# A two-layer hybrid network, second feed-forward: float32 of the norm kept, operands prepared in steps, phases overlapped

## The chip, the cores and the metric

The kernel runs on one core of one Trainium2 chip. The metric is device time in microseconds (us), lower is better. TensorE (PE; PEld are its weight loads), VectorE (DVE), ScalarE (ACT), GpSimd (POOL) and SyncE (SP, which issues the DMAs) run side by side, each with an in-order queue.

## What is computed

The reference is a network of two layers on 1024 latent tokens (and 256 context tokens in the first layer), width 1024. Each layer has a mixer (attention and a recurrence) and a feed-forward part. The change lies in the second layer's feed-forward part and in the norm ahead of it, both on latent tokens only:

```python
def squared_relu_mlp(u, w1, w2):
    return jnp.square(jax.nn.relu(u @ w1)) @ w2

h_l = h_l + mod_l[5] * squared_relu_mlp(
    modulate(rms_norm(h_l, norm2_w[i]), mod_l[3], mod_l[4]), w_ff1[i], w_ff2[i])
return rms_norm(h_l, final_norm_w)
```

`w_ff1` is 1024 x 4096, `w_ff2` 4096 x 1024, all float32.

## The kernel before

Activations stand with features on the 128 partitions and tokens in the free dimension. A float32 number is kept as two rounded float32 parts (hi and lo, type fp32r), and one product of 128 x 128 weights with 512 tokens is three matmuls (`mm3`, lines 132 to 134): hi by hi, hi by lo, lo by hi. Splitting takes a cast on ScalarE and a subtraction on VectorE or POOL (`split`, lines 139 and 140).

`norm_mod` (line 1222) makes the normed input of one half of the tokens (c = 0 or 1, 512 tokens): squares and their sums over eight feature tiles, a matmul with ones (line 1240) and a power on POOL (1243), transposes that spread the result over the partitions (1248), and then `mod_part` for each feature tile k: VectorE's scaling (355), ScalarE's shift that gives hi (356), and lo on VectorE (364), or, for k = 1, 3, 5, 7 of the second half, by a float32 copy (358) and POOL (362). It is a generator; other code advances it step by step, and each step appends to the engines' queues. `out_proj` advances it for the first half, and its last eight steps of squares for the second.

`ff_halves` (line 2441) then does the feed-forward part in three pieces.

- `ff` on four units (1,0,0), (1,1,0), (1,0,1), (1,1,1): an ordinary first product for 512 hidden features, each unit 48 matmuls, result squared and spilled to memory. The first unit goes through k outermost. After each half unit it advances `fills` by `rate` = 7 steps: the rest of the norm, the spilling of the residual (8 steps), and `ff_combine` (line 1460).
- `ff_first` (1504), the seven-product phase for the other hidden features (Winograd's form of Strassen's scheme): features and tokens are halved, and of four blocks of u (B11, B21, B12, B22) and four combinations (T1 to T4) seven are multiplied with seven combinations of four weight blocks. `ff_combine` makes T1 to T4: it adds hi and lo of u together on POOL (1471), forms sums on VectorE and splits them. There are 14 pairs of hidden blocks with 7 products each; a product is 12 matmuls into one PSUM bank. `weights` prepares the weight blocks, FFA = 5 ahead; `post` takes the results from PSUM in steps, makes the seven combinations of the squared hidden values and writes them to memory (`hs_d`).
- `ff_second` (1623), the seven-product phase of the second product: 7 groups of 7 products; a product is four chains of 6 matmuls, each into a bank of its own (8 banks in all). `operands` loads weights (1637) and hidden values (1645), forms the four weight sums (1662 to 1665) when a group's first operand is due, and splits both operands (`pair`). The main loop keeps FFB = 3 operands ahead. After each chain the result of the chain before it is added to U (1709) or to the residual (1716), from a list `posts`.

The last hidden features follow as ordinary products, with the final norm. The order of the work is that of emission (`manual_schedule`): what stands earlier in a queue holds up what stands behind it. Tiles come from pools: slots `S` (45 of 4 KB per partition), temporaries `T` (6), PSUM banks `P` (8).

Of the kernel before, what the change touches and what calls it, by code (L numbers as in the profile page):

```python
# [21 lines left out]
KT = 8  # L22
# [325 lines left out]

def mod_part(E, src, r, u, k, c, gain, shift, pool=False):

    nc = E.nc
    v = 0 if c < 2 else 1
    f = E.T([128, CH[c][1]])
    hi, lo = u.part(k, c, 0), u.part(k, c, 1)
    nc.vector.scalar_tensor_tensor(f, src, gain[:, k, v:v + 1], r, op0=OP.mult, op1=OP.mult)
    nc.scalar.activation(hi, f, AF.Identity, bias=shift[:, k, v:v + 1])  # L356
    if pool:
        nc.scalar.activation(f, f, AF.Identity, bias=shift[:, k, v:v + 1])
    yield
    yield  # L360
    if pool:
        nc.gpsimd.tensor_tensor(lo, f, hi.bitcast(F32), op=OP.subtract)
    else:
        nc.vector.scalar_tensor_tensor(lo, f, shift[:, k, v:v + 1], hi.bitcast(F32), op0=OP.add, op1=OP.subtract)  # L364
    yield
# [128 lines left out]
def drain(g):  # L494
    for _ in g:
        pass
# [724 lines left out]

def norm_mod(E, h, u, c, gain, shift, pool=False, lag=2, which=0):

# [26 lines left out]
    yield from pipe([mod_part(E, h.part(k, c), r[:, :n], u, k, c, gain, shift, k in MPOOL[which][c])  # L1250
                     for k in range(KT)], 1)

# [201 lines left out]
FFA = 5  # L1454
FFB = 3
B11, B21, B22, B12, T1, T2, T3, T4 = range(8)
MOVING = {1: B11, 2: B21, 3: B22, 4: T4, 5: T1, 6: T2, 7: T3}


def ff_combine(E, u, B):  # L1460

    nc = E.nc
    for b, k, c in ((B11, 0, 0), (B21, 4, 0), (B12, 0, 1), (B22, 4, 1)):
        B[b] = [u.tile(k + i, c) for i in range(4)]
    for b in (T1, T2, T3, T4):
        B[b] = []
    f32 = lambda t, i: t[:, i].bitcast(F32)

    def whole(t):
        f = E.T([128, 512], name="uf")  # L1470
        nc.gpsimd.tensor_tensor(f, f32(t, 0), f32(t, 1), op=OP.add)
        return f

    def put(b, f, pool):
        t = E.S([128, 2, 512], F32R, name="ut")
        E.split(t[:, 0], t[:, 1], f, pool=pool)
        B[b].append(t)

    for a, b in ((T1, T2), (T3, T4)):
        for k in range(4):  # L1480
            f12, f22 = whole(B[B12][k]), whole(B[B22][k])
            yield
            d = E.T([128, 512], name="ud")
            if a == T1:
                f11 = whole(B[B11][k])
                nc.vector.tensor_tensor(d, f12, f11, op=OP.subtract)
                nc.vector.tensor_tensor(f22, f22, d, op=OP.subtract)
                yield
                put(T1, d, False)
                yield  # L1490
                put(T2, f22, False)
            else:
                f21 = whole(B[B21][k])
                nc.vector.tensor_tensor(d, f22, f12, op=OP.subtract)
                yield
                put(T3, d, False)
                nc.vector.tensor_tensor(f22, f32(B[T2][k], 0), f32(B[T2][k], 1), op=OP.add)
                nc.vector.tensor_tensor(f21, f21, f22, op=OP.subtract)
                yield
                put(T4, f21, False)  # L1500
            yield


def ff_first(E, l, B, pairs, dst, fills):
# [87 lines left out]
    order = ((1, "x"), (6, "y"), (5, "z"), (7, "y"), (2, "x"), (4, "y"), (3, "z"))  # L1592
    yield
    for i, p in enumerate(pairs):
        bank = {}
# [27 lines left out]
def ff_second(E, l, groups, src, h, fills):  # L1623
# [22 lines left out]

    def pair(raw, pool):
        hi, lo = (E.S([128, 2, 512], F32R, name="sp") for _ in range(2))
        E.split(hi, lo, raw, pool=pool)
        return hi, lo  # L1650

    def operands():
        v = nc.vector
        load(0)
        for j in range(2):
            fetch(j)
        yield
        for j, (i, n) in enumerate(todo):
            if n == 1:
                a11, a21, a22, a12 = (raws.pop((i, m, z)) for m, z in ((0, 0), (0, 1), (1, 1), (1, 0)))  # L1660
                s1, s2, s4 = (E.S([128, 2, 512], name="ws") for _ in range(3))
                v.tensor_tensor(s1, a21, a22, op=OP.add)  # L1662
                v.tensor_tensor(s2, s1, a11, op=OP.subtract)  # L1663
                v.tensor_tensor(a21, a11, a21, op=OP.subtract)  # L1664
                v.tensor_tensor(s4, a12, s2, op=OP.subtract)  # L1665
                A = {1: a11, 2: a12, 3: s4, 4: a22, 5: s1, 6: s2, 7: a21}
                del a11, a12, a21, a22, s1, s2, s4
# [5 lines left out]
            o = [(w, t)]  # L1673
            del w, t
            yield o.pop()

    ops, ready, posts = operands(), [], []
    next(ops)
    yield
    U, banks, hr = {}, {}, None  # L1680
    for i, g in enumerate(groups):
        for n in order:
            while len(ready) < (1 if i == 0 and n == 1 else 2 if i == 0 and n == 2 else FFB):
                x = next(ops, None)
                if x is None:
                    break
                ready.append(x)
                x = None
            w, t = ready.pop(0)
            if n == 1 and i == 0:  # L1690
                hr = h()
            for o in range(4):
# [659 lines left out]
LAG1 = 6  # L2352
# [5 lines left out]
def kernel(ctx: ExitStack, tc: tile.TileContext, A, out, dbg=None, upto=99):  # L2358
# [57 lines left out]
    E.mark('mixer1')  # L2416
    u, W, norm = Act(E, 8), {}, []

    def tail(O, h):
        norm.extend(norm_mod(E, h, u, c, E.gain[1, 1], E.mod[1][:, 3], c == 1, (2, LAG1)[c], 2) for c in range(2))  # L2420
        return out_proj(E, 1, O, h, 0, W, None, norm[0])
# [15 lines left out]
    E.mark('ff1')  # L2437
    ff_halves(E, 1, u, h, norm[1])


def ff_halves(E, l, u, h, fill):
    nc = E.nc
# [19 lines left out]
    drain(fills[0])  # L2462
    del B[B12]
    u.t.clear()
    left = 7 * len(pairs)
    back = Back(E)

    def residual():
        for _ in range(8):
# [74 lines left out]
```

## Time and profile before

| | us |
|---|---|
| median of 3 runs | 3035.26 (3035.12 to 3037.11) |
| the profiled execution, its own time | 3036.59 |
| its span from first to last instruction | 3034.8 |
| busy: PE, DVE, ACT, POOL | 2848.8, 1837.2, 1314.1, 1250.3 |

The span is the time from the first instruction to the last in the profiled execution; times in rows count from its start. Busy time is the union of an engine's instructions. Matmuls overlap in the records (each lasts 0.39 us and the next starts 0.23 us later), so pace is read from starts and counts. "Idle before" is the time for which an engine stood still ahead of an instruction, and behind the arrow stands whose end released it. PEclk is the granted clock of TensorE as a share of 2.4 GHz.

### The profile page before, as it was taken

What the parts mean: (1) busy time and instruction counts of PE and PEld (TensorE: products, weight loads), DVE (VectorE), ACT (ScalarE), POOL (GpSimd) and SP (SyncE); (2) the same over time, 40 slices, a digit from 0 to 9 for tenths busy, and PEclk for the clock granted to TensorE, in tenths of its full rate; (3) what the DMA queues carried; (4) which work ended last, traced back from release to release, by engine and by line L of the source; (5) the groups of instructions that cost most, each with busy time, mean ns of one, the idle gap of its engine ahead of it and who ended that gap; (6) DMA issues with size and microseconds to landing.
All of it is one profiled execution on the core that took longest, in us unless ns stands there. A gap on an engine that the chain in (4) does not pass through costs nothing. (4 is left out here: it accounts for less than half of the span.)

```text
span 3034.8 us, 43217 instructions
## 1 busy us (share of the span) xinstructions
PE 2848.8 (94%) x16181; PEld 2453.1 (81%) x16181; DVE 1837.2 (61%) x3507; ACT 1314.1 (43%) x2475; POOL 1250.3 (41%) x946
## 2 busy tenths in 40 slices
PE   7999999989999999999999989899996699889998
PEld 5797789878888888888888788789885588767777
DVE  5453468876435444444445865898976655567767
ACT  5554468764112121111134444488863344433331
POOL 1443347634223223222233343335446655465560
PEclk9999999999999999999999999999998899989999
DMA  7236689821212122222214212235312344464441
GB/s 254 80 119 202 225 229 233 223 84 61 71 44 70 63 70 74 80 77 70 84 29 142 74 56 87 81 109 159 117 36 111 118 153 153 149 219 139 137 148 56
DMA packets 255801, 355.16 MB, mean 117 GB/s; under 512 B 34848, under 2 KB 160616, under 8 KB 255592
## 3 DMA queue, kind: packets, MB, share of 16 engines
q1 hardware_dynamic: 255592, 352.41, 36.5%
q8 instruction: 127, 2.08, 0.3%
q14 instruction: 82, 0.67, 0.1%
HBM read 261.05 MB, written 91.31 MB: 116 GB/s over the span
## 5 line engine op out<-in xcount | busy, mean ns | idle before, releaser
L132 PE MATMUL ps<-act,whi 128*128 128x512 f32 (+1 forms) x1728 | 630.9, 365 | 6.3 <-ACT act L356 5.2
L133 PE MATMUL ps<-act,whi 128*128 128x512 f32 (+1 forms) x1728 | 627.4, 363 | 6.2 <-DVE act L364 4.4
L134 PE MATMUL ps<-act,wlo 128*128 128x512 f32 (+1 forms) x1728 | 625.1, 362 | 2.1 <-POOL wlo L92 1.1
L92 POOL TENSOR_TENSOR wlo<-wst,whi 128x1024 fp32r<-128x1024 f32 x134 | 333.3, 2496 | 365.4 <-ACT whi L90 242.6
L132 PEld LDWEIGHTS ps<-act,whi 128*128 128x128 f32 x1728 | 329.2, 190 | 60.7 <-issue 7.6
L133 PEld LDWEIGHTS ps<-act,whi 128*128 128x128 f32 x1728 | 329.1, 190 | 55.3 <-DVE act L364 5.8
L134 PEld LDWEIGHTS ps<-act,wlo 128*128 128x128 f32 x1728 | 328.6, 190 | 53.0 <-POOL wlo L92 1.6
L140 DVE TENSOR_TENSOR hid<-t,hid 128x512 fp32r<-128x512 f32 (+1 forms) x104 | 65.5, 630 | 451.8 <-ACT hid L139 451.8
L132 PE MATMUL ps<-hid,whi 128*128 128x512 f32 (+1 forms) x848 | 301.2, 355 | 0.0
L133 PE MATMUL ps<-hid,whi 128*128 128x512 f32 (+1 forms) x848 | 299.6, 353 | 0.0
L134 PE MATMUL ps<-hid,wlo 128*128 128x512 f32 (+1 forms) x848 | 299.4, 353 | 0.0
L1348 POOL TENSOR_TENSOR t<-t 128x512 f32<-128x512 f32 (+1 forms) x104 | 95.7, 920 | 483.5 <-ACT t L1347 475.4
L1347 ACT ACTIVATE t<-ps 128x512 f32<-128x512 f32 (+1 forms) x104 | 55.3, 532 | 491.6 <-PE ps L134 491.6
L1372 DVE SCALAR_TENSOR_TENSOR hl<-ps,mod,hl 128x512 f32<-128x512 f32 (+1 forms) x296 | 208.7, 731 | 63.2 <-PE ps L134 60.1
L724 ACT ACTIVATE sc<-sc,st 128x1024 f32<-128x1024 f32 (+3 forms) x208 | 178.1, 859 | 32.1 <-DVE st L1826 23.1
L132 PE MATMUL ps<-sp,sp 128*128 128x512 f32 x392 | 161.5, 412 | 28.3 <-DVE hl L1716 23.1
L90 ACT CAST whi<-wst 128x1024 fp32r<-128x1024 f32 x138 | 142.1, 1048 | 90.4 <-PE ps L133 41.8
L753 DVE TENSOR_TENSOR pt<-ps,pt 128x512 fp32r<-128x512 f32 (+2 forms) x304 | 169.2, 598 | 17.7 <-ACT pt L752 15.2
L132 PEld LDWEIGHTS ps<-hid,whi 128*128 128x128 f32 x848 | 160.4, 189 | 24.0 <-issue 1.6
L134 PEld LDWEIGHTS ps<-hid,wlo 128*128 128x128 f32 x848 | 160.3, 189 | 22.1
L133 PEld LDWEIGHTS ps<-hid,whi 128*128 128x128 f32 x848 | 160.4, 189 | 21.5
L133 PE MATMUL ps<-sp,sp 128*128 128x512 f32 x392 | 160.1, 408 | 11.3 <-DVE sp L140 7.9
(393 smaller groups left out, 6541.4 us busy)
## 6 DMA issues: line engine op xcount, KB each, us to landing
wm<-in_w_mod SPq DMA_DIRECT2D x96, 512.0 KB
wst<-in_w_ff SPq DMA_DIRECT2D x86, 512.0 KB
hs<-hs_d SPq DMA_DIRECT2D x49, 512.0 KB
wr<-in_w_ff SPq DMA_DIRECT2D x42, 512.0 KB
hs_d<-g SPq DMA_DIRECT2D x42, 512.0 KB
hl<-h_d SPq DMA_DIRECT2D x24, 512.0 KB
wst<-in_w_in_even SPq DMA_DIRECT2D x20, 512.0 KB
wst<-in_w_in_odd SPq DMA_DIRECT2D x18, 512.0 KB
```

Of the source, the lines that this page charges most:

```text
L90: self.nc.scalar.copy(hi, st)
L92: engine.tensor_tensor(lo, st, hi.bitcast(F32), op=OP.subtract)
L132: t.matmul(ps, w[0], u[0], start=start, stop=False, **kw)
L133: t.matmul(ps, w[0], u[1], start=False, stop=False, **kw)
L134: t.matmul(ps, w[1], u[0], start=False, stop=stop, **kw)
L140: (self.nc.gpsimd if pool else self.nc.vector).tensor_tensor(lo, src, hi.bitcast(F32), op=OP.subtract)
L724: self.E.nc.scalar.activation(s, s, AF.Exp, bias=self.nm, accum_out=self.st[:, 5 + i:6 + i])
L753: nc.vector.tensor_tensor(pt[:, :, 1], src, pt.bitcast(F32)[:, :, 0], op=OP.subtract)
L1347: nc.scalar.activation(r, ps[:, :n], AF.Relu)
L1348: nc.gpsimd.tensor_tensor(r, r, r, op=OP.mult)
L1372: nc.vector.scalar_tensor_tensor(dst, ps[:, :n], gate[:, o, v:v + 1], dst, op0=OP.mult, op1=OP.add)
```

## The change

- `mod_part` and `norm_mod` take a dictionary `keep`: for the second layer the float32 value is written to a kept tile (eight slots: k and k + 4 of a half share one), the float32 shift is done for every k, and lo is the difference of the two (VectorE, or POOL as before). The order of k becomes 0, 4, 1, 5, 2, 6, 3, 7.
- `ff_combine` takes these tiles: four sums in a row on VectorE per k, then four splits, lo of T2 and T4 on VectorE, of T1 and T3 on POOL. Three steps per k.
- `fills` now also holds the first six steps of `ff_first` (loads and five weight blocks), and is advanced by FFR = 10 steps instead of 7.
- `operands` of the second phase goes in four steps per operand: cast of the weights, cast of the hidden values, lo of the weights on POOL, lo of the hidden values on POOL (first three operands of a group) or VectorE (the other four; before, POOL had the second, fourth and sixth). The four weight sums of the next group go with the second step of the group's last four operands. The main loop advances it by one step per chain, or two when fewer than FFB = 2 operands are ready.
- The first FFS = 16 steps of the second phase are issued between the last products of the first one, from the 93rd on, and the residual is loaded two tiles per chain of the first product.

```diff
-def mod_part(E, src, r, u, k, c, gain, shift, pool=False):
+def mod_part(E, src, r, u, k, c, gain, shift, pool=False, keep=None):
...
-    f = E.T([128, CH[c][1]])
+    if keep is None:
+        f = E.T([128, CH[c][1]])
+    else:
+        if k % 4 not in keep:
+            keep[k % 4] = E.S([128, 2, 512], name="uf")
+        f = keep[k % 4][:, k // 4]
...
-    if pool:
+    if pool or keep is not None:
         nc.scalar.activation(f, f, AF.Identity, bias=shift[:, k, v:v + 1])
     yield
     yield
-    if pool:
-        nc.gpsimd.tensor_tensor(lo, f, hi.bitcast(F32), op=OP.subtract)
+    if pool or keep is not None:
+        (nc.gpsimd if pool else nc.vector).tensor_tensor(lo, f, hi.bitcast(F32), op=OP.subtract)
...
     yield from pipe([mod_part(E, h.part(k, c), r[:, :n], u, k, c, gain, shift, k in MPOOL[which][c], keep)
-                     for k in range(KT)], 1)
+                     for k in (range(KT) if keep is None else (0, 4, 1, 5, 2, 6, 3, 7))], 1)
...
 FFA = 5
-FFB = 3
+FFR = 10
+FFB = 2
+FFS = 16
...
-def ff_combine(E, u, B):
+def ff_combine(E, u, F, B):
...
+    for k in range(4):
+        a, b = F[0].pop(k), F[1].pop(k)
+        f11, f21, f12, f22 = a[:, 0], a[:, 1], b[:, 0], b[:, 1]
+        d = E.T([128, 512], name="ud")
+        for o, x, y in ((f11, f12, f11), (d, f22, f11), (f12, f22, f12), (f21, f21, d)):
+            nc.vector.tensor_tensor(o, x, y, op=OP.subtract)
+        yield
+        for n, f in ((T2, d), (T1, f11), (T3, f12), (T4, f21)):
+            t = E.S([128, 2, 512], F32R, name="ut")
+            E.split(t[:, 0], t[:, 1], f, pool=n in (T1, T3))
+            B[n].append(t)
+            if n in (T1, T4):
                 yield
...
     yield
+    while len(ready) < FFA:
+        ready.append(next(ws))
+        yield
     for i, p in enumerate(pairs):
...
+        for n in range(4):
+            sums(0, n)
+            yield
         for j, (i, n) in enumerate(todo):
-            if n == 1:
...
-            if n == 5:
+            at = j % 7
+            if at == 0:
                 load(i + 1)
             fetch(j + 2)
-            w = pair(A.pop(n), True)
-            t = pair(moving.pop(j), j % 7 in (1, 3, 5))
...
+            x, y = A[i].pop(n), moving.pop(j)
+            w, t = ([E.S([128, 2, 512], F32R, name="sp") for _ in range(2)] for _ in range(2))
+            nc.scalar.copy(w[0], x)
+            yield
+            nc.scalar.copy(t[0], y)
+            if at > 2 and i + 1 < len(groups):
+                sums(i + 1, at - 3)
+            yield
+            nc.gpsimd.tensor_tensor(w[1], x, w[0].bitcast(F32), op=OP.subtract)
+            del x
+            yield
+            (nc.gpsimd if at in (0, 1, 2) else nc.vector).tensor_tensor(t[1], y, t[0].bitcast(F32), op=OP.subtract)
+            del y
+            ready.append((w, t))
...
+                if n == 1 and i == 0:
+                    hr = h()
+                if n == 1 and i == 0 or len(ready) < FFB:
+                    next(ops, None)
+                next(ops, None)
...
-    fills = [chain(fill, spill(), ff_combine(E, u, B))]
-    del h
-    first = ff_first(E, l, B, pairs, {p: hs[p // 2][:, p % 2] for p in pairs}, fills)
+    first = ff_first(E, l, B, pairs, {p: hs[p // 2][:, p % 2] for p in pairs}, [])
+    fills = chain(fill, spill(), ff_combine(E, u, F, B), islice(first, 1 + FFA))
...
-    ff(E, l, u, None, ops, fill=fills[0], spill=hd, rate=7)
+    ff(E, l, u, None, ops, fill=fills, spill=hd, rate=FFR)
...
-    next(first)
+    left, steps = 7 * len(pairs), 0
     for _ in first:
         left -= 1
-        if left == 4:
-            next(second)
+        if left < 6 and steps < FFS:
+            step(second, 3 if left < 3 else 2)
+            steps += 3 if left < 3 else 2
+    step(second, FFS - steps)
```

## Rows read from the trace of the kernel before

**Rows 1.** The page, part 1: busy time, share, instructions of each engine.

```profile
PE 2848.8 (94%) x16181; PEld 2453.1 (81%) x16181; DVE 1837.2 (61%) x3507; ACT 1314.1 (43%) x2475; POOL 1250.3 (41%) x946
```

**Rows 2.** Stretches: PE, PEld, DVE, ACT, POOL busy (instructions), PEclk, DMA share, GB/s.

```profile
2290.20:2332.90 42.70, 37.28 (x157) 29.05 (x156) 21.27 (x26) 17.12 (x28) 21.61 (x17) 0.92 0.43 172
2332.90:2376.90 44.00, 0.00 (x0) 0.00 (x0) 32.48 (x32) 10.38 (x18) 29.51 (x20) 0.54 0.22 72
2376.90:2646.40 269.50, 269.10 (x1176) 221.57 (x1176) 150.42 (x178) 128.60 (x221) 144.06 (x98) 0.99 0.44 148
2646.40:2659.10 12.70, 0.79 (x2) 0.28 (x1) 11.21 (x10) 3.14 (x4) 2.53 (x1) 0.66 0.61 215
2659.10:2707.90 48.80, 38.27 (x144) 30.38 (x144) 29.60 (x26) 22.54 (x25) 37.01 (x14) 0.85 0.76 282
2883.80:2928.20 44.40, 40.96 (x168) 33.35 (x169) 31.88 (x37) 15.21 (x16) 26.14 (x11) 0.92 0.30 99
...
2974.40:3034.80 60.40, 52.37 (x305) 45.39 (x303) 41.15 (x79) 13.34 (x41) 0.00 (x0) 0.95 0.18 70
...
2382.00:2642.00 260.00, 259.74 (x1146) 214.72 (x1146) 146.58 (x173) 124.59 (x215) 140.99 (x96) 1.00 0.45 153
```

**Rows 3.** Waits from 2290 to 2382: in total, times, longest.

```profile
PE ps L132 <- ACT sw L139: 44.0, 1, 44.0
...
PE ps L133 <- DVE act L364: 4.3, 1, 4.3
```

**Rows 4.** Timeline of PE, DVE, ACT, POOL around the first units: start, length, instruction.

```profile
2290.13 0.95 PE L1240 MATMUL ps<-one,t 128*128 128x1 f32 x8
...
2284.90 3.91 DVE L364 SCALAR_TENSOR_TENSOR act<-t,mod,act 128x512 fp32r<-128x512 f32 x2
...
2299.73 1.40 DVE L355 SCALAR_TENSOR_TENSOR t<-hl,gain,ps 128x512 f32<-128x512 f32 x2
...
2300.50 1.38 ACT L356 ACTIVATE act<-t,mod 128x512 fp32r<-128x512 f32 x2 [1.42 <-DVE t L355]
...
2292.88 1.02 POOL L1243 TENSOR_TENSOR nst<-nst,mhalf 128x4 f32<-128x4 f32 x1 [1.53 <-DVE nst L1242]
2293.87 1.04 POOL L1348 TENSOR_TENSOR t<-t 128x512 f32<-128x512 f32 x1
```

**Rows 5.** Groups by line (count, busy, mean ns, idle before), and VectorE's timeline.

```profile
L1471 POOL TENSOR_TENSOR uf<-act 128x512 f32<-128x512 f32 x24 | 36.9, 1563 | 3.3 <-DVE uf L1498 2.0 <-DVE ut L140 1.3
...
L140 POOL TENSOR_TENSOR sw<-s,sw 128x512 fp32r<-128x512 f32 x28 | 36.2, 1296 | 48.1 <-ACT sw L139 32.3 <-issue 15.7
...
2325.46 1.77 DVE L1486 TENSOR_TENSOR ud<-uf,uf 128x512 f32<-128x512 f32 x1
...
2331.16 0.68 DVE L1486 TENSOR_TENSOR ud<-uf,uf 128x512 f32<-128x512 f32 x1
```

**Rows 6.** Waits of TensorE from 2646 to 2960: in total, times, longest.

```profile
PE ps L132 <- DVE hl L1716: 23.1, 6, 5.9
...
PE ps L132 <- ACT sp L139: 5.2, 2, 4.0
```

**Rows 7.** Timeline of VectorE at a group boundary.

```profile
2742.02 1.22 DVE L1662 TENSOR_TENSOR ws<-wr,wr 128x1024 f32<-128x1024 f32 x1
...
2746.68 3.40 DVE L140 TENSOR_TENSOR sp<-hs,sp 128x1024 fp32r<-128x1024 f32 x1
```

**Rows 8.** Groups of the second phase by line.

```profile
L1716 DVE SCALAR_TENSOR_TENSOR hl<-ps,mod,hl 128x512 f32<-128x512 f32 x140 | 102.3, 746 | 56.1 <-PE ps L134 56.1
...
L140 POOL TENSOR_TENSOR sp<-wr,sp 128x1024 fp32r<-128x1024 f32 x28 | 68.7, 2457 | 73.4 <-ACT sp L139 59.1 <-issue 11.5 <-PE ps L133 2.8
...
L140 DVE TENSOR_TENSOR sp<-hs,sp 128x1024 fp32r<-128x1024 f32 x28 | 57.3, 2046 | 10.9 <-ACT sp L139 10.9
...
L1709 DVE TENSOR_TENSOR u<-ps,u 128x512 f32<-128x512 f32 x52 | 35.9, 690 | 24.7 <-PE ps L134 24.4
```

**Rows 9.** SyncE's timeline: the second group's weight loads.

```profile
2663.03 4.61 SPq L1637 DMA_DIRECT2D wr<-in_w_ff  x4
```

More of the change, by code (lines that the diff above doesn't have):

```diff
@@ L1 @@
 from contextlib import ExitStack
-from itertools import chain
+from itertools import chain, islice
 import numpy as np
@@ L1219, in out_proj, with norm_mod @@
     step(norm)
-def norm_mod(E, h, u, c, gain, shift, pool=False, lag=2, which=0):
+def norm_mod(E, h, u, c, gain, shift, pool=False, lag=2, which=0, keep=None):
     nc = E.nc
@@ L1249, in norm_mod @@
     yield
-    yield from pipe([mod_part(E, h.part(k, c), r[:, :n], u, k, c, gain, shift, k in MPOOL[which][c])
-                     for k in range(KT)], 1)
+    yield from pipe([mod_part(E, h.part(k, c), r[:, :n], u, k, c, gain, shift, k in MPOOL[which][c], keep)
+                     for k in (range(KT) if keep is None else (0, 4, 1, 5, 2, 6, 3, 7))], 1)
 def ff_ops(cs, G=2):
@@ L1466, in ff_combine @@
         B[b] = []
[L1467 to L1487, printed above, removed]
-                yield
[L1489 to L1501, printed above, removed]
+    for k in range(4):
[10 more added lines that the diff above has]
+            if n in (T1, T4):
+                yield
 def ff_first(E, l, B, pairs, dst, fills):
@@ L1645, in fetch, with sums @@
             nc.sync.dma_start(t, src[groups[i]][MOVING[n]].rearrange("a p t -> p a t"))
[L1647 to L1650, printed above, removed]
+    A, ready = {}, []
+    def sums(i, n):
+        v = nc.vector
+        g = A.setdefault(i, {})
+        if n == 0:
+            g[5] = E.S([128, 2, 512], name="ws")
+            v.tensor_tensor(g[5], raws[i, 0, 1], raws[i, 1, 1], op=OP.add)
+        elif n == 1:
+            g[6] = E.S([128, 2, 512], name="ws")
+            v.tensor_tensor(g[6], g[5], raws[i, 0, 0], op=OP.subtract)
+        elif n == 2:
+            g[3] = E.S([128, 2, 512], name="ws")
+            v.tensor_tensor(g[3], raws[i, 1, 0], g[6], op=OP.subtract)
+        else:
+            v.tensor_tensor(raws[i, 0, 1], raws[i, 0, 0], raws[i, 0, 1], op=OP.subtract)
+            for k, m, z in ((1, 0, 0), (2, 1, 0), (4, 1, 1), (7, 0, 1)):
+                g[k] = raws.pop((i, m, z))
     def operands():
-        v = nc.vector
         load(0)
+        yield
         for j in range(2):
@@ L1657, in operands @@
         yield
-        for j, (i, n) in enumerate(todo):
-            if n == 1:
[L1660 to L1667, printed above, removed]
-            if n == 5:
+        yield
[3 more added lines that the diff above has]
+            yield
+        for j, (i, n) in enumerate(todo):
+            at = j % 7
+            if at == 0:
                 load(i + 1)
             fetch(j + 2)
-            w = pair(A.pop(n), True)
-            t = pair(moving.pop(j), j % 7 in (1, 3, 5))
-            o = [(w, t)]
-            del w, t
[L1675 to L1679, printed above, removed]
+            x, y = A[i].pop(n), moving.pop(j)
+            w, t = ([E.S([128, 2, 512], F32R, name="sp") for _ in range(2)] for _ in range(2))
+            nc.scalar.copy(w[0], x)
+            yield
+            nc.scalar.copy(t[0], y)
+            if at > 2 and i + 1 < len(groups):
+                sums(i + 1, at - 3)
+            yield
+            nc.gpsimd.tensor_tensor(w[1], x, w[0].bitcast(F32), op=OP.subtract)
+            del x
+            yield
+            (nc.gpsimd if at in (0, 1, 2) else nc.vector).tensor_tensor(t[1], y, t[0].bitcast(F32), op=OP.subtract)
+            del y
+            ready.append((w, t))
+            del w, t
+            yield
+    ops, posts = operands(), []
+    for _ in range(FFS):
+        next(ops)
+        yield
     U, banks, hr = {}, {}, None
@@ L1682, in ff_second @@
         for n in order:
[L1683 to L1688, printed above, removed]
             w, t = ready.pop(0)
-            if n == 1 and i == 0:
-                hr = h()
             for o in range(4):
@@ L2416 @@
     E.mark('mixer1')
-    u, W, norm = Act(E, 8), {}, []
+    u, W, norm, F = Act(E, 8), {}, [], [{}, {}]
     def tail(O, h):
-        norm.extend(norm_mod(E, h, u, c, E.gain[1, 1], E.mod[1][:, 3], c == 1, (2, LAG1)[c], 2) for c in range(2))
+        norm.extend(norm_mod(E, h, u, c, E.gain[1, 1], E.mod[1][:, 3], c == 1, (2, LAG1)[c], 2, F[c])
+                    for c in range(2))
         return out_proj(E, 1, O, h, 0, W, None, norm[0])
@@ L2437, with ff_halves @@
     E.mark('ff1')
-    ff_halves(E, 1, u, h, norm[1])
-def ff_halves(E, l, u, h, fill):
+    ff_halves(E, 1, u, F, h, norm[1])
+def ff_halves(E, l, u, F, h, fill):
     nc = E.nc
@@ L2455, in spill @@
             yield
-    fills = [chain(fill, spill(), ff_combine(E, u, B))]
-    del h
-    first = ff_first(E, l, B, pairs, {p: hs[p // 2][:, p % 2] for p in pairs}, fills)
+    first = ff_first(E, l, B, pairs, {p: hs[p // 2][:, p % 2] for p in pairs}, [])
+    fills = chain(fill, spill(), ff_combine(E, u, F, B), islice(first, 1 + FFA))
+    del h, fill
     ops = [(1, 0, 0), (1, 1, 0), (1, 0, 1), (1, 1, 1)]
-    ff(E, l, u, None, ops, fill=fills[0], spill=hd, rate=7)
-    drain(fills[0])
+    ff(E, l, u, None, ops, fill=fills, spill=hd, rate=FFR)
+    drain(fills)
     del B[B12]
     u.t.clear()
-    left = 7 * len(pairs)
     back = Back(E)
     def residual():
-        for _ in range(8):
+        for _ in range(2):
             back.lat()
```

## The prediction

> **What bounds the kernel now.** The page comes first: TensorE is 94% busy over the span [rows 1], so the question is where the rest lies in the stages that the diff touches. The view by stretches answers it [rows 2]. Undisturbed, 1146 matmuls take 260.00 us, 0.2269 us each. The first seven-product phase is 1176 matmuls in 269.5 us, already at that rate. Ahead of it TensorE does nothing for 44.0 us, and the stretch before that (four units of the ordinary first product) takes 42.7 us. After it come 12.7 us with two matmuls. The second phase is again 1176 matmuls, 266.8 us at the full rate, but runs from 2646.4 to 2974.4, 328.0 us: 61.2 us lost. A group of 168 matmuls should take 38.1 us and takes 44.4 at a granted clock of 0.92.
>
> The waits name who came last. The 44.0 us end at the split of the first weight block, which stands behind the whole combination in the in-order queues [rows 3]. In the second phase, ahead of which ScalarE's splits are waited for too, most waits end at the update of the residual (line 1716) on VectorE, 23.1 us in six waits, one per group boundary [rows 6]. The timeline shows why: four sums (lines 1662 to 1665) and a split of 3.40 us run in a row, about 8 us, while PSUM results wait behind them [rows 7]. Of a group's 6.3 us of loss 3.4 are that wait (the row with six waits, one of them 5.9) and 2.8 the slow stretch after it, in which the granted clock has fallen from 2.4 to 1.2 GHz.
>
> **The change, part by part.** The sum is made against the profiled execution, 3036.59 us, 1.3 us above the median of the runs shown (3035.26).
>
> *Norm.* Twelve more activations on ScalarE, by 0.7 us each (two in 1.38, [rows 4]), 8.4 us: eight for the first column half, four for the second. ScalarE is busy 17 of 42.7 us there [rows 2]; VectorE, which waits for them, is later than they are, so hidden. The order 0, 4, 1, 5, 2, 6, 3, 7 is not free. The unit (1,0,0) reads k = 0, 1, 2, 3 in steps of six matmuls (1.36 us), ends where line 1240 starts (2290.13, [rows 4]) and so begins at 2279.2 (48 matmuls), so k = 3 is wanted at 2283.5; it now is the seventh to be made, and the seventh's low part lies in the middle of the pair at 2284.90 to 2288.81 [rows 4], about 2286.9. That is +3.4 us. Bounds: 0 (VectorE keeps up) and 5.
>
> *FFR 7 to 10.* With ten steps per tick the transposes of the second half's norm are issued in the second tick, straight behind the eight tiny matmuls of line 1240 (end 2291.08), with no unit between. Their input comes from POOL at 2293.90 [rows 4]: +2.8 us, and TensorE's queue has the next unit behind them. In exchange line 355 starts some 3.4 us sooner relative to that point, and the 5.4 us of waits for these halves (one of 4.3 stands in [rows 3]) shrink to about 3. With the slow stretch of two short waits (2 us) and without that of the long one (2 us), the four units end at about 2336 instead of 2332.9.
>
> *Combination.* Gone: 24 additions on POOL, 36.9 us [rows 5]. VectorE has per k four sums and two splits instead of five and four: 24 instead of 36; POOL gets 8 splits by 1.3 us. It is issued in the fourth and fifth tick, beside the units, and the five first weight blocks behind it in ticks five and six, with their four loads from SP. What decides is when the first block is split. From the first line 355 (again about 2299.7, since it moves by -3.4 and +3.4) until then, POOL has 3 squares by 1.04 [rows 4], 4 splits of the norm, 8 of the combination and 1 of the weights by 1.3: 20 us. VectorE has 4 + 3 + 24 operations with two SBUF inputs by 0.68, 21 us. These two do not overlap freely: line 1486 takes 0.68 us while POOL is idle and 1.77 beside it [rows 5]. Taken one after the other they make 41 us, 2341; with some 3 us in which unit results go ScalarE, POOL, ScalarE, VectorE and block the queues, **2344**. If they overlapped fully the block would be ready by 2331 and TensorE would not wait after 2336. Before, POOL's additions took 1.54 us in such company against 1.3 for a split; by that ratio 41 becomes 49, and with 5 us of queue waits it would be 2354. I take 2344, since the row of 1.77 us is the state in which the combination runs. The Trainium skill, "SBUF — State Buffer", section "Who interferes with whom", gives this as a rule: a VectorE instruction with two SBUF inputs and a GpSimd instruction that reads SBUF exclude each other for a whole instruction. By that rule the sum is the 2344 above, without it 2336; the row agrees with it.
>
> The first phase then starts at 2344 instead of 2376.9, a gain of 33, less 2 us for its fourth product, whose weights are split behind a unit's result: **-31 us**.
>
> *Seam of the phases.* The sums and the first splits are issued from the 93rd product on, in VectorE's gaps: sixteen steps are spread over the last five products. Loads on SP keep their place (nothing is issued between), so the sums may wait for the weights and hold the results of the last products behind them; those banks are not wanted at once. Both splits of the first operand are POOL's, 5 us [rows 8], done about 1 us after the last product. Price now 12.7 us; then 1 (bounds 0 and 4).
>
> *First group.* Waits for splits (ScalarE's in [rows 6]) and slow stretches cost some 10 us: 48.8 us for 144 matmuls [rows 2], less 32.7 and the 5.9 of the boundary. POOL has two splits for each of the first three operands, 5 us a product of 5.45; the residual's eight loads now go two per chain, between the other fetches, and line 1716 waits for them with the sums behind it; the next group's four weight loads are issued some 20 us sooner than at 2663.03 [rows 9] (behind product 96) and share the DMA. I take 7 left (bounds 3 and 10).
>
> *Group boundaries.* No work goes away: VectorE has 28 results (20 by 0.75, 8 by 0.69), four sums by 1.2 and four splits by 2.05, 33.6 us of 38.1 [rows 7, 8]; POOL stays at 26. But one sum now falls into each of four products. Such a product has 3.0 + 1.2 + 2.05 = 6.2 us for VectorE against 5.45 for TensorE: four of them leave it some 3 us late, and the other three products, 2.9 us each, make that good. A chain may reuse its bank three chains (4.1 us) after the result was ready, so 3 us of lag is just borne. With splits of 3.4 us each time it is not, and 3 to 4 us would be waited. I take 1.5 us a boundary instead of 6.3; bounds 0 and 6.3. Six boundaries: 9 us.
>
> The second phase then takes 266.8 + 1 + 7 + 9 = 284 us instead of 328: **-44 us**. Sum: -31 - 44 = -75, so about 2960. The last part, from 2974.4, is unchanged.
>
> **The rivals.**
> 1. *VectorE still sets the group.* Its work per group is the same, and if its splits meet POOL each time (3.40 in [rows 7]) the wait only moves inside the group. For it: 33.6 of 38.1 us. Against: products with one sum instead of four. Only seams and first group are won, 31 + 12 + 3 = 46: 2989. Chance 0.15.
> 2. *All is hidden*: the combination is ready before the units end and the groups run at 38.1. 40 + 56 = 96: 2938. For it: TensorE's first phase runs so already, with VectorE busy 56%. Against: the 1.77 us of line 1486. Chance 0.14.
> 3. *The first seam does not close*: early weight blocks or operands wait for slots of a pool that is now fuller (eight float32 tiles are kept), and the change does not do what it says there. Then 44 and some 6 are won: 2985. The queues speak for it, the freed residual tiles against. Chance 0.06.
> 4. *Slower*: short waits in each product in place of one long one per group, at the banks into which a second product adds while VectorE has not yet read the first. The clock gives the price: each wait is followed by about 2.8 us of slow matmuls, if a short one has the same effect. With waits of 1 us at every product but one of a group (six, 3.8 us each) a group costs 23 instead of 6.3, +16.7 by seven, +117; less the seams' 46: 3106. It decides from about 3.4 such waits a group, (46 / 7 + 6.3) / 3.8. For it: VectorE is 0.8 us a product too slow in four products. Against: it is that only while results are late, and the other three products have 2.5 us to spare each. Chance 0.06, of which 0.01 near the break-even.
>
> **How the numbers follow.** The forecast, 2960, has 0.59. Its own bounds are 2934 (40 at the first seam, 61 in the second phase) and 2993 (22 and 20). The range 2934 to 2990 takes in rivals 1 to 3 and leaves out rival 4 and the ends. A measurement of this kernel can tell about 0.2% (6 us) from no change. Faster by more: 0.59 + 0.15 + 0.14 + 0.06 = 0.94; within it 0.01; slower 0.05.
>
> **What would show it.** Right: the wait of 44.0 us shrinks to under 12 and still ends at a weight block or an operand; the first phase keeps its 269 us; between the phases under 2 us are idle; sums stand single in VectorE's timeline, and waits for line 1716 sum to under 8 us instead of 23.1; groups of 38 to 40 us. New: a wait of some 3 us each at k = 3 of the first unit and at line 1248. Wrong: groups still at 44 (rival 1), granted clock under 0.9 in all groups (rival 4), or a first weight block after 2360 (rival 3).

## The result, and the profile after

The changed kernel takes 2964.73 us (median of four runs, 2961.4 to 2966.33) against 3036.19 of the kernel before: ratio 0.9761, interval 0.9744 to 0.9778, 71.5 us less. Forecast: 2960. The profiled execution has a span of 2962.4 us against 3034.8, so its stages account for 72.4 us. One line of the page, part 1, answers to [rows 1]:

```profile
PE 2839.0 (96%) x16181; PEld 2445.5 (83%) x16181; DVE 1814.2 (61%) x3495; ACT 1321.2 (45%) x2487; POOL 1233.7 (42%) x930
```

The same number of matmuls, 96% of a shorter span. The stretches show where (columns as in [rows 2]): the four units, the gap, the first phase, its body; then the first group of the second phase, the other groups, and one group of these:

```profile
2291.70:2335.30 43.60, 38.16 (x157) 30.19 (x155) 24.78 (x35) 22.44 (x38) 18.54 (x15) 0.92 0.55 205
2335.30:2342.18 6.88, 0.00 (x1) 0.00 (x1) 5.96 (x8) 3.13 (x6) 4.30 (x3) 0.67 0.00 0
...
2342.18:2623.98 281.80, 272.98 (x1176) 224.70 (x1177) 158.52 (x185) 134.31 (x230) 153.78 (x105) 0.97 0.45 154
2372.00:2623.00 251.00, 251.00 (x1109) 207.85 (x1108) 145.33 (x171) 122.76 (x211) 135.12 (x91) 1.00 0.47 160
2623.98:2662.00 38.02, 31.77 (x122) 24.05 (x121) 33.47 (x28) 18.37 (x23) 33.63 (x13) 0.87 0.92 343
2662.00:2902.10 240.10, 239.78 (x1058) 197.82 (x1057) 197.56 (x228) 84.38 (x84) 161.95 (x61) 1.00 0.44 147
...
2738.20:2776.30 38.10, 38.10 (x170) 31.55 (x169) 31.98 (x36) 14.04 (x15) 26.83 (x11) 1.00 0.46 152
```

The idle 44.0 us have become 6.88. But the first phase now takes 281.8 us, 15.0 more than 1176 matmuls at 0.2269 us; since its body has TensorE busy for 251.00 us of 251.00, all 15.0 lie in its first 30 us. It ends at 2624.0 instead of 2646.4: 22.4 us won. The second phase takes 278.1 us (2624.0 to 2902.1) instead of 328.0: 49.9 us won. It is 11.3 above 266.8, nearly all of it in the first group (38.02 us for the 121 matmuls that start in it, granted clock 0.87); the others run at 38.1 us. The last part, 60.3 us, is as it was.

The waits of TensorE from 2290 to 2905, columns as in [rows 3]:

```profile
PE ps L132 <- ACT sw L139: 6.9, 1, 6.9
PE ps L132 <- DVE g L1543: 6.5, 1, 6.5
PE ps L132 <- ACT sp L1678: 3.6, 1, 3.6
PE ps L1253 <- POOL nst L1248: 2.9, 1, 2.9
PE ps L132 <- DVE hl L1723: 2.8, 2, 2.4
PE ps L134 <- POOL sw L140: 2.3, 1, 2.3
PE ps L133 <- POOL act L367: 1.6, 1, 1.6
PE ps L132 <- ACT act L361: 0.8, 1, 0.8
```

Line 1723 is the old line 1716: 2.8 us instead of 23.1 [rows 6]. New is the second line, 6.5 us for line 1543 (old 1556), which reads a PSUM bank in the first phase. The timeline of PE, VectorE, ScalarE and POOL shows what it stands behind (start, length, engine, instruction, and the idle time before it with its releaser):

```profile
2354.54 1.29 POOL L140 TENSOR_TENSOR sw<-wr,sw 128x512 fp32r<-128x512 f32 x1
2355.78 1.04 POOL L1353 TENSOR_TENSOR t<-t 128x512 f32<-128x512 f32 x1
...
2356.86 0.62 ACT L139 CAST hid<-t 128x512 fp32r<-128x512 f32 x1 [2.63 <-POOL t L1353]
...
2357.51 0.69 DVE L140 TENSOR_TENSOR hid<-t,hid 128x512 fp32r<-128x512 f32 x1 [5.01 <-ACT hid L139]
2359.78 0.69 DVE L140 TENSOR_TENSOR hid<-t,hid 128x512 fp32r<-128x512 f32 x1 [1.58 <-ACT hid L139]
2360.39 1.76 DVE L1527 TENSOR_TENSOR wr<-wr,s 128x512 f32<-128x512 f32 x1
2362.08 0.68 DVE L1543 TENSOR_TENSOR g<-ps,p 128x512 f32<-128x512 f32 x1
...
2362.81 0.80 PE L132 MATMUL ps<-ut,sw 128*128 128x512 f32 x1 [6.50 <-DVE g L1543]
```

These are still results of the ordinary units, which ended at 2335.1. Each goes ScalarE (1352), POOL (the square, 1353), ScalarE (cast), VectorE (split). The square (2355.78) stands behind a weight split on POOL, ScalarE is idle for 2.63 us until it can cast, VectorE stands 5.01 us for the cast, and behind it stand a second such split, a weight sum and, last, the read of the bank into which the fourth product adds. That product's weights are not what is late: POOL has split them at 2354.59, and TensorE stands still from 2356.31.

In the second phase the timeline of VectorE at the boundary that answers to [rows 7]:

```profile
2751.12 1.40 DVE L1645 TENSOR_TENSOR ws<-wr,wr 128x1024 f32<-128x1024 f32 x1
2752.44 1.49 DVE L1716 TENSOR_TENSOR u<-ps,u 128x512 f32<-128x512 f32 x2
2753.84 1.22 DVE L1685 TENSOR_TENSOR sp<-hs,sp 128x1024 fp32r<-128x1024 f32 x1
...
2755.95 0.75 DVE L1723 SCALAR_TENSOR_TENSOR hl<-ps,mod,hl 128x512 f32<-128x512 f32 x1 [0.30 <-PE ps L134]
```

Each sum and each split now stands between results, and VectorE is idle again before 2755.95: it has caught up within the product.

### The profile page after: what moved, and what is told of

It is laid out like the page before. It is cut to its first block, busy times and chain, and to the rows that moved or that the text cites. A ratio compares the mean times of both kernels' runs of the same rounds, so it can differ in the third digit from the quotient of the medians.

```text
span 2962.4 us, 43182 instructions
## 1 busy us (share of the span) xinstructions
PE 2839.0 (96%) x16181; PEld 2445.5 (83%) x16181; DVE 1814.2 (61%) x3495; ACT 1321.2 (45%) x2487; POOL 1233.7 (42%) x930
## 5 line engine op out<-in xcount | busy, mean ns | idle before, releaser
L757 ACT CAST pt<-ps 128x512 fp32r<-128x512 f32 (+2 forms) x304 | 153.4, 526 | 35.7 <-PE ps L744 28.4
L132 PE MATMUL ps<-sp,sp 128*128 128x512 f32 x392 | 154.3, 394 | 6.3 <-ACT sp L1678 3.6
```

Source lines behind the costliest of these rows:

```text
L132: t.matmul(ps, w[0], u[0], start=start, stop=False, **kw)
L757: nc.scalar.copy(pt[:, :, 0], src)
```

## The experiments

Each run's median is given; "changed" is the changed kernel, 2964.73. The part of the kernel ahead of line 1245, which the edits hardly touch, ends up to 7 us apart in the profiled executions (2285.8 to 2293.1); where stages are compared, they are counted from the last matmul of that line to the end of the first phase (331.6 us changed, 355.4 before). So counted, the four runs that leave this stretch as it is (2, 3 and both of 7) agree with the changed kernel within 0.2 us, so a difference of 1 us can be told there, which the medians cannot do. The second phase is counted from its first matmul to the first of the last part (278.1 us changed).

**1. Only the second phase and the seam.** The kernel before, with the changed second phase:

```diff
 (norm, combination and first phase of the kernel before, rate=7)
-FFB = 3
+FFB = 2
+FFS = 16
...
+        if left < 6 and steps < FFS:
+            step(second, 3 if left < 3 else 2)
```

> Norm, combination and first phase as in the kernel before, second phase and seam as changed. Theory (the two halves of the change add up): the first seam costs 44.0 us again, so of the 71 us won about 50 stay (278 instead of 328 us from the first phase's end to the second's), time near 2987. Rival (the spread steps pay only because less work stands in the queues after the new combination): second phase above 290 us, time above 3000.

Measured: 2989.82, ratio 0.984 (0.9825 to 0.9854). First phase 355.3 us from line 1245, as before; second phase 278.5, as changed. Its waits, same columns:

```profile
PE ps L132 <- ACT sw L139: 44.0, 1, 44.0
PE ps L132 <- DVE hl L1734: 6.3, 2, 3.8
```

The 44.0 us are back, the boundary waits are not. The halves are independent: 48 us (3038.18, the kernel before in the same runs, less 2989.82) belong to the second phase with its seam, 25 (2989.8 less 2964.7) to the first.

**2. The four sums in a row again**, everything else changed:

```diff
-            if at > 2 and i + 1 < len(groups):
-                sums(i + 1, at - 3)
+            if at == 6 and i + 1 < len(groups):
+                for q in range(4):
+                    sums(i + 1, q)
```

> As changed, but the four weight sums of the next group stand in a row with the group's last operand instead of one each with the last four. Theory (the row of sums holds back the results of PSUM): a wait for line 1723 of 2 to 4 us returns at each of six boundaries with a slow stretch behind it, +15 to +36 us, 2980 to 3000. Rival (what pays is that casts and splits are spread over the chains): within 4 us of 2965.

Measured: 3016.69, ratio 0.9932 (0.9915 to 0.9948), 52 us above changed, more than the 15 to 36 forecast. Waits of TensorE, and VectorE's timeline at a boundary:

```profile
PE ps L132 <- DVE hl L1724: 47.0, 8, 9.7
```

```profile
2695.41 2.65 DVE L1645 TENSOR_TENSOR ws<-wr,wr 128x1024 f32<-128x1024 f32 x1
2698.15 1.23 DVE L1648 TENSOR_TENSOR ws<-ws,wr 128x1024 f32<-128x1024 f32 x1
...
2702.61 3.35 DVE L1653 TENSOR_TENSOR wr<-wr,wr 128x1024 f32<-128x1024 f32 x1
```

The sums hold results back for 10.5 us (2695.41 to 2705.89), two of those shown at two to three times the 1.23 of the other. The second phase takes 332.0 us, no less than the 328 of before: without the spreading of the sums the rest of the change wins nothing there.

**3. An operand's four steps at once**, at the first chain of a product:

```diff
-                if n == 1 and i == 0 or len(ready) < FFB:
-                    next(ops, None)
-                next(ops, None)
+                if o == 0:
+                    for _ in range(8 if n == 1 and i == 0 or len(ready) < FFB else 4):
+                        next(ops, None)
```

> As changed, sums spread, but the four steps of an operand are issued together at a product's first chain. Theory (the row of sums was the cause, a sum and one split together are under the 4.1 us that a bank can wait): 0 to +6 us, 2965 to 2971. Rival (the spreading over chains is what pays): waits at each product, +15 us or more.

Measured: 2992.63, ratio 0.985 (0.9835 to 0.9864), 28 us above changed; second phase 306.7. The wait of TensorE, and VectorE's timeline ahead of one of the seven:

```profile
PE ps L132 <- DVE hl L1723: 23.8, 7, 6.3
```

```profile
2735.50 3.00 DVE L1653 TENSOR_TENSOR wr<-wr,wr 128x1024 f32<-128x1024 f32 x1
2738.42 3.39 DVE L1685 TENSOR_TENSOR sp<-hs,sp 128x1024 fp32r<-128x1024 f32 x1
2741.74 2.71 DVE L1723 SCALAR_TENSOR_TENSOR hl<-ps,mod,hl 128x512 f32<-128x512 f32 x4
```

As many microseconds of waiting as before the change (23.1, [rows 6]), although the sums are one per product. The theory that the spread of the sums is all falls. With its steps issued together a product's sum and split stand next to each other; where both meet POOL they take 6.4 us, no result is read in them, and four are behind them at 2741.74. The place of the steps between the chains matters as much as the spread of the sums.

**4. The combination's low parts all on VectorE:**

```diff
-            E.split(t[:, 0], t[:, 1], f, pool=n in (T1, T3))
+            E.split(t[:, 0], t[:, 1], f, pool=False)
```

> As changed, but the low parts of T1 and T3 are made on VectorE instead of POOL: eight operations of 0.7 us on VectorE for eight of 1.3 to 1.7 on POOL. Theory (the two engines exclude each other in these operations, so the sum of both counts): the first weight block is split 3 to 5 us sooner, 2960 to 2962. Rival (they overlap and VectorE alone sets the pace): it is split 3 to 6 us later, 2968 to 2971.

Measured: 2956.11, ratio 0.973 (0.9715 to 0.9744), 8.6 us below changed. From line 1245 to the end of the first phase it takes 326.0 us instead of 331.6, so 5.7 us come from this stretch; that the edit wins more than these is not shown. Counted from that line the first product starts 3.7 us sooner, and its third matmul, which needs the low part of the first block, 5.8 us sooner; part of it is lost again, as the wait for line 1543 grows from 6.5 to 8.3 us. Timelines of VectorE and POOL, of the changed kernel and then of this one:

```profile
2322.65 1.77 DVE L1481 TENSOR_TENSOR uf<-uf,uf 128x512 f32<-128x512 f32 x1
...
2320.48 3.40 POOL L140 TENSOR_TENSOR ut<-uf,ut 128x512 fp32r<-128x512 f32 x2 [3.96 <-ACT ut L139]
```

```profile
2316.62 1.89 DVE L140 TENSOR_TENSOR ut<-uf,ut 128x512 fp32r<-128x512 f32 x3
2318.43 0.69 DVE L1481 TENSOR_TENSOR uf<-uf,uf 128x512 f32<-128x512 f32 x1
```

VectorE does two splits more per k, three in 1.89 us, and the sum behind them takes 0.69; in the changed kernel POOL has 3.40 for these two, and a sum beside them takes 1.77. From one k to the next it is 4.94 us (second sums at 2314.21 and 2319.15) instead of 5.93 (2318.53 and 2324.46). VectorE's six operations of the changed kernel, 0.61 us from start to start, and POOL's two, 1.28 each without company, make 6.2 us one after the other; side by side VectorE alone would need 3.7. Work moved onto the busier engine made the pair faster. That is the exclusion on which the 2344 rested, tested by an edit: the Trainium skill, "SBUF — State Buffer", section "Who interferes with whom", states it for VectorE instructions with two SBUF inputs beside GpSimd instructions that read SBUF, and these rows agree with it.

**5. The square of the units' results on ScalarE**, so that POOL is no stop on their way:

```diff
-            nc.gpsimd.tensor_tensor(r, r, r, op=OP.mult)
+            if rate:
+                nc.scalar.activation(r, r, AF.Square)
+            else:
+                nc.gpsimd.tensor_tensor(r, r, r, op=OP.mult)
```

> As changed, but in the four ordinary units the square is taken on ScalarE instead of POOL, so that a unit's result goes ScalarE, ScalarE, ScalarE, VectorE. Theory (in-order queues: each such result holds ScalarE and VectorE for a round through POOL, and the first post of the new phase, line 1543, waits behind the last two): the first block is split 2 to 4 us sooner and the wait of 6.5 us at line 1543 falls under 3, together -5 to -9 us, 2956 to 2960. Rival (the amount of work on VectorE and POOL sets the time, not the rounds): the eight squares of 1.04 us leave POOL, but the wait stays, 0 to -3 us.

Measured: 2952.83, ratio 0.9723 (0.971 to 0.9737), 11.9 us below changed, more than the 5 to 9 forecast; 319.0 us from line 1245 to the end of the first phase instead of 331.6. Counted from that line the first product starts 5.7 us sooner, and the wait for line 1543 shrinks. That wait (here for line 1546), and ScalarE's timeline where the changed kernel had 2.63 us of idle time ahead of the cast:

```profile
PE ps L132 <- DVE g L1546: 2.8, 1, 2.8
```

```profile
2347.12 0.63 ACT L1354 ACTIVATE t<-t 128x512 f32<-128x512 f32 x1
2347.78 0.62 ACT L139 CAST hid<-t 128x512 fp32r<-128x512 f32 x1
```

The square is followed by the cast at once, and the wait for the bank falls from 6.5 to 2.8 us. So most of it was the units' results on their way over POOL, not the weights of the fourth product. Behind the 2.8 us the granted clock is 1.00, behind the 6.5 us of the changed kernel thirteen matmuls follow at the lower level; that is part of the gain.

**6. The order of k, plain again** (the high and low parts of the norm made in the order 0 to 7):

```diff
-                     for k in (range(KT) if keep is None else (0, 4, 1, 5, 2, 6, 3, 7))], 1)
+                     for k in range(KT)], 1)
```

> As changed, but the norm makes k in the order 0 to 7. As predicted before the result (the unit reads k in this order, so the changed order costs 3.4 us at k = 3): -3 to -5 us. Rival (VectorE is ahead enough, the trace after shows 0.25 us there and 2.4 us at the second half): -2 to 0 us, and the first weight block not sooner, since the combination begins behind the whole norm either way.

Measured: 2961.77, ratio 0.9749 (0.9735 to 0.9762). 3.0 us below changed, within what can be told from no change. From line 1245 on it takes 329.6 against 331.6 us. The 3.4 us that I had charged for the order at k = 3 are not there. The first product starts as late as before (49.8 us behind line 1245 in both), as the rival had it; the 2 us are won behind that, in the first phase, where the wait for line 1543 is 5.2 instead of 6.5 us. Why it is shorter stays open.

**7. The order at the second seam, and the first group's splits on VectorE.** Two runs for the 11 us of the first group. The changed kernel counts 2, 4, 6, 9, 12, 15, 18 steps at the seam, two more than the sixteen of FFS, so the first chains of the second phase are issued ahead of the first phase's last combinations. Capped at sixteen, they come behind:

```diff
-            step(second, 3 if left < 3 else 2)
-            steps += 3 if left < 3 else 2
+            m = min(FFS - steps, 3 if left < 3 else 2)
+            step(second, m)
+            steps += m
```

> As changed, but the last steps of the first phase's results are issued before the second phase's first product, not after its second. Theory (these sums, 2.9 us each beside POOL, hold up line 1723 at 2648, and tiles not yet written to memory hold up ScalarE's casts at 2651): the waits of 2.44 and 3.56 us in the first group go, -3 to -6 us. Rival (memory traffic is the limit there, 0.92 of the DMA engines, and the residual's loads now stand behind the last writes): 0 to +6 us.

The other takes the first group's low parts of the moving operands off POOL:

```diff
-            (nc.gpsimd if at in (0, 1, 2) else nc.vector).tensor_tensor(t[1], y, t[0].bitcast(F32), op=OP.subtract)
+            (nc.gpsimd if at in (0, 1, 2) and i > 0 else nc.vector).tensor_tensor(t[1], y, t[0].bitcast(F32), op=OP.subtract)
```

> As changed, but in the second phase's first group the low parts of the first three hidden operands are made on VectorE (1.2 us alone) instead of POOL (2.4). Theory (the first group waits for line 1723 because POOL runs without a pause there and VectorE's two-input operations stand still beside it, 2.8 to 3.4 us each): the 7 to 8 us of waits fall under 3, -4 to -8 us, 2957 to 2961. Rival (VectorE's amount of work is the limit there): three more operations, +2 to +5 us. Rival 2 (memory traffic, 0.92 of the DMA engines): no difference.

Measured: 2963.59, ratio 0.9758 (0.9745 to 0.9771), and 2966.25, ratio 0.9765 (0.9752 to 0.9778); second phases 278.9 and 279.1. Neither differs from changed, so both theories fall: in the first run the two waits are 2.27 and 4.69 us instead of 2.44 and 3.56. What the timeline of the changed kernel shows in that stretch is this:

```profile
2640.33 2.89 DVE L1564 TENSOR_TENSOR g<-g,g 128x512 f32<-128x512 f32 x1
...
2635.93 6.74 POOL L1682 TENSOR_TENSOR sp<-ws,sp 128x1024 fp32r<-128x1024 f32 x2
```

The first phase's last combinations (lines 1564 to 1569) run beside POOL's splits, this one in 2.89 us where an undisturbed one takes 0.68 (line 1568, at 2645.95). In the first run line 1564 comes at 2627.24, and three of the four still take 2.8 to 2.9 us. With POOL relieved (the second run) the waits for line 1723 are even longer, 7.0 us in this stretch. The three splits moved to VectorE take 1.43, 2.58 and 2.83 us there, not the 1.2 of the theory, because POOL's weight splits go on beside them. That VectorE and POOL together have too much there is consistent with both runs. But the transfers are in the chain too. ScalarE's longest idle times in this stretch, in the changed kernel and in the first run, end at a DMA:

```profile
2651.51 1.04 ACT L1676 CAST sp<-wr 128x1024 fp32r<-128x1024 f32 x1 [6.90 <-DMA hs_d<-g]
```

```profile
2644.83 1.05 ACT L1678 CAST sp<-hs 128x1024 fp32r<-128x1024 f32 x1 [10.78 <-DMA hs<-hs_d]
```

In the changed kernel TensorE's wait of 3.56 us ends at the cast that follows the first of these (2653.25). Neither run takes traffic away, so the cause of these 11 us stays open.

**8. The first weight blocks ahead of the combination:**

```diff
-    fills = chain(fill, spill(), ff_combine(E, u, F, B), islice(first, 1 + FFA))
+    fills = chain(fill, spill(), islice(first, 1 + FFA), ff_combine(E, u, F, B))
```

> As changed, but the first five weight blocks are loaded and split ahead of the combination instead of behind it. Theory (queue order: TensorE waits for a weight block behind the combination): the first product starts at the end of the units, 7 us sooner, and the second product waits for T2, -3 to -7 us in all. Rival (amount of work: all of it is needed by the second or third product): the wait only moves one product on, within 2 us of 2965.

Measured: 2963.3, ratio 0.9758 (0.9745 to 0.9772). The first product now follows the units without a gap, at 2333.7, and the longest waits of TensorE are these:

```profile
PE ps L132 <- ACT ut L139: 8.3, 2, 4.3
```

The wait for the block became a wait for the second product's operand (ut). From line 1245 to the end of the first phase it takes 329.0 us, 2.6 less than changed: between the theory and the rival. Most of what was late is the work of both, not its order.

**9. Edits 4 and 5 together:**

```diff
-            E.split(t[:, 0], t[:, 1], f, pool=n in (T1, T3))
+            E.split(t[:, 0], t[:, 1], f, pool=False)
...
+            if rate:
+                nc.scalar.activation(r, r, AF.Square)
```

> Squares of the units on ScalarE and all low parts of the combination on VectorE, together. If the two act on different waits (rounds of a unit's result through POOL; exclusion of the two engines) they add up: -20 us against the changed kernel, 2943 to 2947. If both only relieve POOL, the second adds little: 2950 to 2953.

Measured: 2948.91 (2944.46 to 2951.11), ratio 0.9707 (0.9694 to 0.972): 15.8 us below changed and ahead of both given kernels. By the medians this lies between the two forecasts. By the stretch from line 1245 to the end of the first phase it is the second: edit 4 alone wins 5.7 us there, edit 5 alone 12.6, both 13.4 (318.2 us). On top of edit 5 the low parts on VectorE are worth 0.8 us. The first product starts 2.4 us sooner than in run 5, but the wait for the bank is 5.0 instead of 2.8 us. So the two do not act on different waits: what one wins at the first block is waited for at the fourth product. Its waits:

```profile
PE ps L132 <- DVE hl L1726: 5.8, 2, 3.4
PE ps L132 <- DVE g L1546: 5.0, 1, 5.0
```

**10. The ticks, on top of 9.** Seven steps in the first two ticks and thirteen in the later ones, so that the transposes come after a unit; and the same with edit 8:

```diff
+            given.append(0)
-            tick(rate if rate else (TICK1 if pace == PACE0 else 2 * pace + 1) if c < 2 else int(pace))
+            tick((rate - 3 if len(given) < 3 else rate + 3) if rate else (TICK1 if pace == PACE0 else 2 * pace + 1) if c < 2 else int(pace))
```

> Squares on ScalarE and low parts on VectorE as in the two together, and the first two ticks have 7 steps, the later ones 13 instead of 10. Theory (the transposes behind line 1240 hold TensorE 2.6 us because no unit stands between): that wait goes, the norm of the second half starts about 1.6 us later, -1 to -3 us against the two together (2949): 2946 to 2948. Rival (VectorE's queue sets the first product's start, and the norm starts later): 0 to +2 us.

> The same with the first five weight blocks ahead of the combination. Theory (with less work in the queues the order counts): the first product starts where the units end, -2 to -5 us against the run without it. Rival (the wait moves on to the second product's operand): within 2 us of it.

Measured: 2949.21, ratio 0.9712 (0.9699 to 0.9725), and 2951.55, ratio 0.9723 (0.971 to 0.9737). No gain over 9: from line 1245 to the end of the first phase 317.6 and 320.7 us, against 318.2. With edit 8 it is 3 us more than without, which neither theory nor rival had. The waits of the first of the two:

```profile
PE ps L133 <- POOL act L367: 2.9, 2, 1.6
...
PE ps L133 <- DVE act L367: 1.0, 1, 1.0
PE ps L132 <- ACT act L361: 0.9, 2, 0.5
```

The transposes are waited for no more, but the norm of the second column half, which has six steps fewer in the first two ticks, is: 2.9 + 1.0 + 0.9 = 4.8 us.

## Why the prediction held, and where it did not

The forecast was 2960, the time is 2964.7; the sum has two errors of opposite sign in it (8.6 us too much at the first seam, 5.9 too little in the second phase), so its closeness is partly luck and says less than its steps. (It starts from 3035 us, as do the rivals' sums, not from the 3036.59 that the prediction names.)

- *Norm.* The wait at k = 3, taken as 3.4 us, is 0.23 us in the trace (its low part starts at 2284.21, and the matmul at 2284.94). I kept the old pace of 3.91 us a pair, a row in which POOL works beside VectorE. Here POOL has just ended (2284.13) and the split takes 0.67 us; the next one, beside POOL, takes 1.55. So VectorE keeps up, my lower bound, in part by chance. Plain order (run 6) finds nothing at k = 3; its 2 us lie behind the first product's start.
- *FFR.* The wait at the transposes, taken as 2.8, is 2.95; the second half's waits, taken as 3, are 2.4 (0.8 + 1.6). The units end at 2335.1, forecast 2336.
- *Combination.* The first block was forecast for 2344. The first matmul runs at 2342.2, the third, which needs the low part, at 2345.7. The sum of both engines' work taken one after the other was the right model for the combination: run 4 moves POOL's part to VectorE, and the low part is there 5.8 us sooner, counted from line 1245. That the number is so close is luck as well. From the first scaling of the second half to the end of that low part it takes 47.9 us, not 44.3, but it begins at 2297.8, not 2299.7. For unit results in the queues 3 us were charged; 47.9 less the 41 of work leaves some 7, and VectorE stands still for 11.9 us (4.52, 4.55 and 2.84) ahead of three of their splits, while POOL works in a part of it.
- *"Less 2 us for its fourth product"* is the term that failed. I saw that this product is held behind a unit's result, but took its weights for what is late, and charged 2 us. What it waits for is the read of its bank (line 1543), which stands in VectorE's queue behind the splits of the last two unit results; it is a wait of 6.50 us, with 2.33 for the first block's low part ahead of it and slow matmuls behind both. The first phase costs 281.8 us where 271.5 were forecast, 10.3 more (less 1.8 for the earlier start): the first seam gains 22.4 instead of 31. Run 5 shows what most of it was made of: the way of the unit's result over POOL.
- *Seam of the phases.* Taken as 1 us, it is 0.3 (the steps are spread over the last six products, not five).
- *First group.* Taken as 7 us, it is some 10, at the upper bound. Cause open (run 7).
- *Group boundaries.* Taken as 9 us for six, they are under 1 in all. I charged each split 2.05 us and each sum 1.2; at the boundary shown three of the four splits take 1.2 us and the sums 1.40 to 2.44, and a group needs 31.98 us of VectorE, not 33.6. The lag that I thought would just be borne is borne with room. The second phase gains 49.9 instead of 44.
- *The rivals.* VectorE does not set the group (rival 1: 44 us a group against 38.1). Not all is hidden (rival 2) at the seam, but in the second phase it came to nearly that. The first seam closes to 6.9 us (rival 3: 44 stay). No short waits in each product (rival 4). Run 2 shows the price of a long one at each boundary: 47 us in eight waits, 52 us in all.
- *The signs.* The 44 us fell under 12, sums stand single, waits for line 1716 are under 8, groups are 38. "The first phase keeps its 269 us" did not hold: 281.8.

## What to carry to other kernels

When a stage is moved forward beside another, follow the *last results of the stage it joins* through every queue: here one engine fewer on their way (the square on ScalarE) was worth 11.9 us, the most of all single edits. In this combination VectorE's instructions with two SBUF inputs and POOL's added up nearly as if on one engine (5.93 us a k for 6.2 of work), and taking work off POOL won 5.7 us although VectorE got it. Two such gains need not add up: the second was worth 0.8 us once the first had been had, because the wait moved on to the next thing that was late. Work for later that is spread one instruction per chain can be free on an engine that is busy 32 of 38 us, while the same instructions in a row cost 52 us.

## What was not expected of the hardware

- How long VectorE's instructions with two SBUF inputs can take beside POOL's: not only 1.77 instead of 0.69 us at 128x512 (line 1481; [rows 5] had that), but up to 2.9 (line 1564), and 3.35 against 1.23 at 128x1024 (lines 1653 and 1648 of run 2).
- How little the length of a wait says of the clock behind it. Two waits of nearly the same length: in the changed kernel, behind 89 matmuls without one, and in run 5 (TensorE's rows, then stretches, columns as above).

```profile
2648.07 0.63 PE L132 MATMUL ps<-sp,sp 128*128 128x512 f32 x1 [2.44 <-DVE hl L1723]
2648.07:2650.50 2.43, 2.43 (x6) 1.66 (x6) 2.43 (x2) 0.00 (x0) 1.51 (x1) 0.55 1.00 329
```

```profile
2353.28 0.50 PE L132 MATMUL ps<-ut,sw 128*128 128x512 f32 x1 [2.79 <-DVE g L1546]
2353.28:2357.00 3.72, 3.72 (x16) 3.10 (x17) 2.87 (x3) 1.14 (x2) 3.65 (x3) 1.00 0.87 285
```

Behind 2.44 us the granted clock is 0.55, near the level of 1.2 GHz; behind 2.79 us it is 1.00, that of 2.4 GHz, and so it is behind one of 3.43 us in run 8 (2359.96). What decides between them is not shown. In the first phase of the changed kernel the waits are followed by the lower level, as here:

```profile
2346.00:2351.00 5.00, 5.00 (x12) 3.85 (x13) 0.22 (x1) 2.08 (x4) 3.52 (x3) 0.50 0.01 3
```

This stretch stands behind the wait of 2.33 us at 2345.72, with the 6.88 us only two matmuls ahead of it. Of the first phase's 15.0 us, 8.8 are its two waits (2.33 and 6.50) and the other 6.2 the matmuls at the lower level behind the waits of 6.88, 2.33 and 6.50: there a wait costs more than its length.
